# A two-layer encoder on one core: splitting the second output weights in the first attention, and multiplying part of the second output projection under the last head

## The chip, the cores and the metric

The kernel is one program on one core of a Trainium2 chip. The metric is device time in microseconds, from start to end of one execution; the median of three runs is 2327.5 us (2325.5 to 2328.0).

## The reference

One sequence of 1024 tokens with 1024 features passes two layers. Each layer is a token mixer and a SwiGLU feed-forward block, each followed by a residual and a layer norm. Layer 0 mixes with multi-head latent attention (8 heads), layer 1 with differential attention (8 heads, two softmax maps each). Both are masked by chunks of 64 tokens.

```
h = x
# layer 0
h = layernorm(ALPHA * h + mla_mixer(h) )          # ends with  o @ mla_w_o
h = layernorm(ALPHA * h + swiglu(h))
# layer 1
#   a = softmax(q0 k0) - lam * softmax(q1 k1);  o = a @ v, per head
#   o = rmsnorm(o, g_sub) * (1 - lambda_init)
h = layernorm(ALPHA * h + o @ diff_w_o)
h = layernorm(ALPHA * h + swiglu(h))
```

All is float32; the output must agree with a float32 computation.

## The kernel before

**Products.** Each float32 operand is split into an upper half `h`, its value rounded to float32r (a cast on ScalarE), and a lower half `l`, the rest (a subtraction on VectorE or GpSimd). A product is three float32r matmuls: `h*h`, `h*l`, `l*h`. `load_w` (L133 to L138) does this for weights: it loads 512 KB into a raw tile of the ring `wr` (two buffers), casts to `wh` and subtracts to `wl` (three buffers each). These rings serve all weights of the attentions.

**Order.** The program is written as a list of steps. A planner at compile time orders the instructions of every engine: it runs a model of the machine, and whenever an engine is free in it, the ready instruction that stands earliest in the program is placed next (some steps are raised in priority). On the chip each engine then takes its instructions in that fixed order; waits are by semaphore. Tiles come from pools of fixed buffers. A tile whose pool is full waits until an older tile's last reader is done.

**Attention.** `attention` runs over 64 steps, 8 heads by 8 blocks of 128 query tokens; the last head takes its blocks in the order 6, 7, 4, 5, 2, 3, 0, 1 (`LAST_ORDER`). At step b it issues `score` for step b + 2 (scores on TensorE, bias and row minimum on VectorE at L220, exponential on ScalarE at L223, scaling on GpSimd at L1024 or L1164, in layer 1 the combination of the two maps on VectorE at L1165), `turn` (transposes on TensorE at L149 and the split of their result at L244 and L245), every second step `mix` (probabilities times values, L256), and then whatever the table `fill` holds for that step. `fill` holds the projections of the next head, so that TensorE has work between the dependent steps of a block. The last head has no next head; its `fill` holds only the per-head norms (`norm_b`, `norm_b2`, L1189 to L1201). In layer 1 a head's normed output goes to DRAM (`o_dr`, L1204), except the last head's, which stays in the tile `bo`.

**Output projection.** `out_proj` loads and splits the eight heads' weights (6 in own tiles, 2 in the rings, for layer 1). Then, for each block of 128 tokens in `LAST_ORDER`, it fetches the block's head outputs from `o_dr` (`of`, L308), scales and splits them (L316, L317), loads the residual input (`z`, L320), multiplies two halves of 512 columns with 24 matmuls each (L144 to L146), adds them to `ALPHA * z` with row sums (L328), normalizes (`layer_norm`, L167 to L185), and transposes the block before for the feed-forward stage (`raw_x`). In layer 1 the split input `oh` and the pair `zy` (z and the normed y) are tiles of the ring `big`, which has five buffers of 1 MB. In the second attention these hold two query tiles, two key tiles and `bo`. As `out_proj` comes after `attention` in the program, the planner places its weight splits early, as soon as buffers are free, and its products when all seven stored heads of a block are in DRAM.

**After it** comes the feed-forward stage: gate and up products first (`gates`, which need the transposed first four blocks), with weights split in the rings.

Of the kernel before, what the change touches and what calls it, by code (L numbers as in the profile page):

```python
# [9 lines left out]
F32 = mybir.dt.float32  # L10
# [6 lines left out]
P = 128  # L17
# [25 lines left out]
def trunk(  # L43
# [82 lines left out]
    def small(name, n=1):  # L126
        return sp.tile([P, 2], F32, tag="small", name=name, bufs=22)[:, :n]

    def load_w(src, cols, name, hi=None, lo=None, eng=None, raw=None):

        if raw is None:
            raw = wp.tile([P, 1024], F32, tag="wr", bufs=2, name=f"r_{name}")
        nc.sync.dma_start(raw[:, :cols], src)  # L133
        if hi is None:
            hi = wp.tile([P, 1024], F32R, tag="wh", name=f"h_{name}")
            lo = wp.tile([P, 1024], F32R, tag="wl", name=f"l_{name}")
        A.copy(hi[:, :cols], raw[:, :cols])
        (eng or G).tensor_tensor(lo[:, :cols], raw[:, :cols], f32(hi[:, :cols]), ALU.subtract)  # L138
        return hi, lo
# [11 lines left out]
    def bcast_row(pool, src, n, name, tag):  # L151
        t = pool.tile([P, n], F32, tag=tag, name=name, bufs=1)
        nc.gpsimd.dma_start(t, src.partition_broadcast(P))
        return t
# [121 lines left out]
                fn()  # L276
        mix(blocks[-1][0], blocks[-1][1] // 2)

    def out_proj(side, w_o, o_dram, x_src, x_dst, lng, lnb, xo, layer, scale=None, last=None):


        with tc.tile_pool(name=f"op{layer}", bufs=2, side=side, reuse_waits="tile") as pool:
            g = bcast_row(pool, lng, D, f"mg{layer}", "g")
            b = bcast_row(pool, lnb, D, f"mb{layer}", "b")
            in_big, in_ring = ((0, 1, 2, 3, 7), (4, 5)) if layer == 0 else ((), (6, 7))
            wo = []
            for h in range(H):
                dst = ()
                if h in in_big:
                    t = big_tile(f"wo{layer}_{h}")  # L290
                    dst = (t[:, 0], t[:, 1])
                elif h not in in_ring:
                    t = pool.tile([P, 2, D], F32R, tag=f"wo{h}", name=f"wo{layer}_{h}", bufs=1)
                    dst = (t[:, 0], t[:, 1])
                wo.append(load_w(w_o[h], 1024, f"wo{layer}_{h}", *dst))

            def pair(name, dt, tag):
                if layer:
                    return big_tile(name, dt)
                return pool.tile([P, 2, D], dt, tag=tag, name=name)  # L300

            prev = None
            for tb in LAST_ORDER:
                nm = f"a{layer}_{tb}"
                of = pool.tile([P, H, P], F32, tag="of", name=f"of_{nm}", bufs=2)
                n = H if last is None else H - 1
                src = o_dram[tb // 2][:n, :, (tb % 2) * P:(tb % 2) * P + P]
                nc.sync.dma_start(of[:, :n], src.rearrange("h p q -> p h q"))  # L308
                ot = pair(f"oh_{nm}", F32R, "oh").rearrange("p a (h q) -> p a h q", h=H)
                oh, ol = ot[:, 0], ot[:, 1]  # L310
                if scale is None:
                    A.copy(oh, of)
                    V.tensor_tensor(ol, of, f32(oh), ALU.subtract)
                else:
                    for hs, o in ((slice(0, H - 1), of[:, :H - 1]), (H - 1, last(tb))):
                        A.activation(oh[:, hs], o, AF.Copy, scale=scale)  # L316
                        V.scalar_tensor_tensor(ol[:, hs], o, scale, f32(oh[:, hs]), ALU.mult, ALU.subtract)  # L317
                zy = pair(f"zy_{nm}", F32, "zy")
# [12 lines left out]
                if tb == LAST_ORDER[-1] and not layer:  # L331
                    y = big_tile(f"y_{nm}", F32)[:, 0]
                layer_norm(z, sums, junk, y, g, b, nm, x_dst[tb * P:(tb + 1) * P, :])
                if prev is not None:
                    raw_x(prev[1], xo, prev[0], f"a{layer}_{prev[0]}")
                prev = (tb, y)
        return lambda: raw_x(prev[1], xo, prev[0], f"a{layer}_{prev[0]}")

    def raw_x(y, xo, tb, name):

# [30 lines left out]
    def split(dst, src, eng):  # L371
        hi, lo = dst
        A.copy(hi, src)  # L373
        eng.tensor_tensor(lo, src, f32(hi), ALU.subtract)  # L374
# [436 lines left out]
        return new, rest, normed  # L811

    o_dr = [[dr.tile([H, P, 256], F32, name=f"o_dr{l}_{g}") for g in range(4)] for l in range(2)]
    xs_dr = [dr.tile([S, D], F32, name=f"xs_dr{l}") for l in range(3)]


# [120 lines left out]
    with ast as st:  # L937
# [64 lines left out]
        def k_nope(h, hf):  # L1002
# [9 lines left out]
            A.copy(kh[:, hs], m)  # L1012
            V.tensor_tensor(kl[:, hs], m, f32(kh[:, hs]), ALU.subtract)

        def score_a(h, i):
            hf, c = i // 4, slice((i % 4) * P, (i % 4) * P + P)
            (qh, ql), (kh, kl), qq = qn[h, hf], kn[h], qr[h, hf]
            l, r = softmax_block(
                lp,
                [(qh[:, c], kh), (qh[:, c], kl), (ql[:, c], kh), (qq[:, c], kr1), (qq[:, c], kr2)],  # L1020
                ba, i, MLA_SCALE, f"a{h}_{i}",
            )
            n = (i + 1) * P
            G.tensor_scalar(l[:, :n], l[:, :n], r, 1.0, ALU.mult, ALU.mult)  # L1024
            lt[h, i] = l
# [13 lines left out]
        def at(slot, fn, *args):  # L1039
            fill.setdefault(slot, []).append(lambda: fn(*args))  # L1040
# [21 lines left out]

    banks("ps2", PS_BUFS)
# [14 lines left out]
        return new_xT(pool, "f0")  # L1078

    xo, stacks = x_pools("m0", "right")  # L1080
    pending = out_proj("left", w_o_a, o_dr[0], x, xs_dr[0], ln_mix_g[0], ln_mix_b[0], xo, 0)
    xT, rest, normed = ffn("left", xo, stacks, pending, 0, xs_dr[0], xs_dr[1], ln_ffn_g[0], ln_ffn_b[0], next_x)


    banks("ps3", PS_BUFS_B)
    with ExitStack() as st:
# [104 lines left out]
        def norm_b2(h, g0=0, g1=4):  # L1191
            parts = []
            for i, (sq, o) in enumerate(sqs.pop((h, g0))):
                m = ps_s(f"ms{h}_{g0}_{i}")[:, :sq.shape[1]]
                T.matmul(m, ones, sq, start=True, stop=True)
                parts.append((sq, o, m))
            for r, _, m in parts:
                A.activation(r, m, AF.Ln, bias=eps_rms, scale=1.0)
            for r, o, _ in parts:
                A.activation(r, r, AF.Exp, scale=-0.5)  # L1200
                G.tensor_tensor(o, o, r, ALU.mult)  # L1201
            if h < H - 1:
                for g in range(g0, g1):
                    nc.sync.dma_start(o_dr[1][g][h], o_rows(h, g))  # L1204

# [39 lines left out]
        at(8 * H - 5, norm_b2, H - 1, 3, 4)  # L1245
        at(8 * H - 4, norm_b, H - 1, 2, 3)
        at(8 * H - 3, norm_b2, H - 1, 2, 3)
        attention(score_b, turn_b, mix_b, fill, 2, (0, 60))
        norm_b(H - 1, 0, 2)
        norm_b2(H - 1, 0, 2)  # L1250

    xst.close()
    xo, stacks = x_pools("m1", "left")
    pending = out_proj("right", w_o_b, o_dr[1], xs_dr[1], xs_dr[2], ln_mix_g[1], ln_mix_b[1], xo, 1, gs, last_rows)
# [91 lines left out]
```

## Time and profile before

| | us |
|---|---|
| median of three runs | 2327.5 (2325.52 to 2328.03) |
| profiled execution, its own time | 2323.21 |
| its span, first to last instruction | 2321.4 |
| TensorE busy | 2255.9 |
| VectorE, ScalarE, GpSimd busy | 1556.4, 1017.1, 891.7 |

The stages on the span's clock, from the timeline: first attention from about 100 to 365, first output projection and feed-forward to about 1105, second attention to 1587 (its last head from about 1525), second output projection to 1670, second feed-forward to the end. The granted clock of TensorE is 0.991 of full speed on average.

A row of a group reads: line, engine, operation, output from input, shapes and count, then durations. "[3.08 <-DVE mx_b L220]" behind a row means that the engine was idle for 3.08 us ahead of it, and what ended that. A row of waits reads: engine and tile that waited, what it waited for, then total us, count and longest. PE is TensorE, DVE VectorE, ACT ScalarE, POOL GpSimd, SP the queue that issues most transfers.

### The profile page before, as it was taken

Reading aid. Unit: us, or ns where it says so; the run is one execution under the profiler, and the core shown is the slowest. Engines: PE = TensorE matmul, PEld = TensorE weight load, DVE = VectorE, ACT = ScalarE, POOL = GpSimd, SP = SyncE. Lnnn points to the kernel's source line nnn. Section 1 sums busy time; section 2 is a strip of 40 time slices with the busy share of each in tenths; the row PEclk is TensorE's granted clock in tenths of the full one; section 3 lists DMA queues with packets and bytes.
Section 4 is the critical chain, followed back from the end, with each engine's and each line's share of the span. In section 5 each row is a group of like instructions: output and inputs, shape, how many; then the busy total and the mean of one; then the engine's idle time right before and its main releaser. Section 6 shows DMA issues by size and latency. Waiting matters only on the chain. (4 is left out here: it accounts for less than half of the span.)

```text
span 2321.4 us, 31073 instructions
## 1 busy us (share of the span) xinstructions
PE 2255.9 (97%) x11410; PEld 1922.3 (83%) x11410; DVE 1556.4 (67%) x2872; ACT 1017.1 (44%) x2089; POOL 891.7 (38%) x696
## 2 busy tenths in 40 slices
PE   7999999999999999999999999989999999999997
PEld 7899997888888887888888898867888888887886
DVE  4566765596666668767476666575596656658777
ACT  4355664352333324445365656564442333324353
POOL 3122342004444455555432424261014444436564
PEclk9999999999999999999999999989999999999999
DMA  5001124344313138454220212133334322337453
GB/s 201 9 28 37 40 71 169 104 164 145 136 68 136 69 118 321 183 185 154 91 55 19 69 37 69 37 110 129 134 138 149 105 99 106 109 131 301 148 198 124
DMA packets 100346, 272.56 MB, mean 117 GB/s; under 512 B 7504, under 2 KB 31184, under 8 KB 90464
## 3 DMA queue, kind: packets, MB, share of 16 engines
q1 hardware_dynamic: 95776, 260.14, 31.7%
q0 software_dynamic: 4416, 10.42, 1.7%
q8 instruction: 90, 1.47, 0.2%
q14 instruction: 64, 0.52, 0.1%
HBM read 197.13 MB, written 69.21 MB: 115 GB/s over the span
## 5 line engine op out<-in xcount | busy, mean ns | idle before, releaser
L373 ACT CAST op_g<-gr 128x512 fp32r<-128x512 f32 x240 | 147.5, 622 | 410.6 <-PE gb L418 229.7
L374 POOL TENSOR_TENSOR op_g<-gr,op_g 128x512 fp32r<-128x512 f32 x104 | 145.9, 1409 | 303.5 <-DVE tmp L509 153.5
L374 DVE TENSOR_TENSOR op_h<-rh,op_h 128x512 fp32r<-128x512 f32 x154 | 162.5, 1085 | 70.3 <-ACT op_h L373 70.3
L418 PE MATMUL ga<-xh_m,op_g 128*128 128x512 f32 x512 | 168.0, 389 | 0.0
L373 ACT CAST op_h<-rh 128x512 fp32r<-128x512 f32 x154 | 92.7, 619 | 145.5 <-DMA rh<-h_dr 38.2
L686 PE MATMUL dw<-op_w_t,op_h 128*128 128x512 f32 x660 | 151.3, 390 | 0.0
L686 PEld LDWEIGHTS dw<-op_w_t,op_h 128*128 128x128 f32 x660 | 123.6, 188 | 25.8 <-DVE op_h L374 0.3
L374 POOL TENSOR_TENSOR op_w_t<-tt,op_w_t 128x512 fp32r<-128x512 f32 x66 | 99.3, 1508 | 79.3 <-ACT op_w_t L373 79.3
L223 ACT ACTIVATE l_b<-l_b,mx_b 128x256 f32<-128x256 f32 (+7 forms) x128 | 99.5, 777 | 69.0 <-DVE mx_b L220 66.9
L686 PE MATMUL dx<-op_w_b,op_h 128*128 128x512 f32 x528 | 122.4, 391 | 6.1 <-ACT op_w_b L373 3.9
L686 PEld LDWEIGHTS dx<-op_w_b,op_h 128*128 128x128 f32 x528 | 98.4, 188 | 29.8 <-ACT op_w_b L373 4.7
L1164 POOL TENSOR_SCALAR l_b<-l_b,r_b,cst 128x128 f32<-128x128 f32 (+3 forms) x64 | 53.0, 827 | 178.5 <-DVE r_b L225 169.7
L418 PE MATMUL gb<-t4h_f,op_g 128*128 128x512 f32 x352 | 115.9, 390 | 3.4 <-DVE tmp L501 3.4
L418 PE MATMUL gc<-b22h_f,op_g 128*128 128x512 f32 x352 | 115.6, 389 | 1.3 <-ACT op_g L373 1.3
L374 DVE TENSOR_TENSOR op_g<-gr,op_g 128x512 fp32r<-128x512 f32 x136 | 109.6, 807 | 9.4 <-ACT op_g L373 9.0
L418 PE MATMUL gc<-t1h_f,op_g 128*128 128x512 f32 x352 | 115.5, 389 | 0.0
L418 PE MATMUL gb<-t3h_f,op_g 128*128 128x512 f32 x352 | 115.2, 389 | 0.0
L418 PE MATMUL gb<-t2h_f,op_g 128*128 128x512 f32 x352 | 114.8, 389 | 0.0
L418 PEld LDWEIGHTS ga<-xh_m,op_g 128*128 128x128 f32 x512 | 96.1, 188 | 19.9
L374 POOL TENSOR_TENSOR op_g<-s,op_g 128x512 fp32r<-128x512 f32 x40 | 55.6, 1391 | 142.9 <-ACT op_g L373 142.9
L144 PE MATMUL bp<-xT_f,h_wb 128*128 128x512 f32 x256 | 102.8, 402 | 0.0
L146 PE MATMUL bp<-xT_f,l_wb 128*128 128x512 f32 x256 | 101.6, 397 | 0.0
(350 smaller groups left out, 6833.8 us busy)
## 6 DMA issues: line engine op xcount, KB each, us to landing
gr<-in_w_gu SPq DMA_DIRECT2D x44, 1024.0 KB, 6.7
rh<-h_dr SPq DMA_DIRECT2D x28, 1024.0 KB, 5.1
h_dr<-sh SPq DMA_DIRECT2D x22, 1024.0 KB, 4.9
h_dr<-hp SPq DMA_DIRECT2D x22, 768.0 KB, 4.1
tt<-in_w_dn SPq DMA_DIRECT2D x22, 512.0 KB, 8.2
rh<-h_dr SPq DMA_DIRECT2D x14, 768.0 KB, 4.5
z<-xs_dr SPq DMA_DIRECT2D x16, 512.0 KB, 10.6
rw_b<-in_w_dn SPq DMA_DIRECT2D x8, 1024.0 KB, 8.9
```

What stands on the lines that cost most here:

```text
L144: T.matmul(ps_out, lh, rh, start=(i == 0), stop=False)
L146: T.matmul(ps_out, ll, rh, start=False, stop=(i == n - 1))
L223: A.activation(l[:, :n], l[:, :n], AF.Exp, bias=mx, scale=-1.0, accum_out=sm)
L373: A.copy(hi, src)
L374: eng.tensor_tensor(lo, src, f32(hi), ALU.subtract)
L418: T.matmul(o, w[:, a, kc], x[b][:, k, :], start=(first and k == 0 and (a, b) == (0, 0)), stop=(k == 3 and a == 1), skip_group_check=True,)
L686: T.matmul(o, h[:, a, c], w[:, b_], start=(first and (a, b_) == (0, 0)), stop=(last and a == 1), skip_group_check=True,)
L1164: G.tensor_scalar(l1[:, :n], l1[:, :n], r1, nlam, ALU.mult, ALU.mult)
```

## The change

1. **Weights of the second output projection.** `split_wo(h)` is put into the first attention's `fill`, one per head (steps 5, 13, ... 53, and 44 for the last): it loads and splits one head's weights through the same rings, and writes both halves to DRAM (`wo_dr`, 1 MB a head). Later they are loaded as finished operands, by GpSimd's queue.
2. **`out_proj`** serves layer 0 alone. For layer 1 there is a class `OutProj`. It is opened at step 54 of the second attention, when the projections are done and the transposed input is released: it issues eight heads' operand loads and fetches the first block's six heads.
3. **Early products.** For the first two blocks (6 and 7) the products of heads 0 to 5 are put into the last head's `fill`: `early` for block 6 at steps 56, 57 and 58 (two heads each), for block 7 at steps 60 and 61 (three heads each). Their sums are added to `ALPHA * z` at once; heads 6 and 7 follow in `late`, at step 63 for block 6, which adds them with the row sums.
4. **Heads 6 and 7 stay on the core** in `bo` (before, head 7 alone), so `o_dr` has six heads.
5. **Buffers.** For the first two blocks the split inputs lie in the weight rings (block 6) and an own tile (block 7), and z in the `wr` ring, where y overwrites it. For the other six blocks `oh` and `zy` are tiles of `big`, as before. The norm's scale and shift, before two tiles of `out_proj`'s pool, are one tile of `big` (`gb1`).

The core of the diff (the cuts in `out_proj` for layer 1's options are left out):

```diff
+    class OutProj:
+        HEADS = H - 2
+        def __init__(self, side, w_dr, o_dram, o_here, x_src, x_dst, scale):
...
+            self.of(LAST_ORDER[0])
+            for h in range(H):
+                if h < self.HEADS:
+                    t = self.pool.tile([P, 2, D], F32R, tag=f"wo{h}", name=f"wo1_{h}", bufs=1)
+                    nc.gpsimd.dma_start(t, w_dr[h])
...
+                else:
+                    t = [wp.tile([P, D], F32R, tag=f"w{p}", name=f"w{p}o1_{h}") for p in "hl"]
+                    for p in range(2):
+                        nc.gpsimd.dma_start(t[p], w_dr[h][:, p])
...
+        def of(self, tb):
+            nm, n = f"a1_{tb}", self.HEADS
+            of = self.pool.tile([P, n, P], F32, tag="of", name=f"of_{nm}")
...
+            nc.sync.dma_start(of, src.rearrange("h p q -> p h q"))
+            first = tb in LAST_ORDER[:2]
+            if tb == LAST_ORDER[0]:
+                hl = [wp.tile([P, D], F32R, tag=f"w{p}", name=f"o{p}_{nm}") for p in "hl"]
+            elif first:
+                t = self.pool.tile([P, 2, D], F32R, tag="oh", name=f"oh_{nm}", bufs=1)
...
+            else:
+                t = big_tile(f"oh_{nm}")
...
+            self.split(tb, slice(0, n), of)
+            if first:
+                z = wp.tile([P, D], F32, tag="wr", name=f"z_{nm}", bufs=2)
+                self.z[tb] = (z, z)
+            else:
+                zy = big_tile(f"zy_{nm}", F32)
...
+            nc.sync.dma_start(self.z[tb][0], self.x_src[tb * P:(tb + 1) * P, :])
...
+        def early(self, tb, heads):
+            for nh in range(2):
+                self.product(tb, nh, heads, heads[-1] == self.HEADS - 1)
+            if heads[-1] == self.HEADS - 1:
+                for nh in range(2):
+                    self.added(tb, nh, ALPHA, False)
+                    del self.m[tb, nh]
+
+        def late(self, tb):
+            self.split(tb, slice(self.HEADS, H), self.o_here(tb))
+            first = tb in LAST_ORDER[:2]
+            for nh in range(2):
+                self.product(tb, nh, range(self.HEADS if first else 0, H), True)
+                self.added(tb, nh, 1.0 if first else ALPHA, True)
+
+        def rest(self, lng, lnb, xo):
+            gb = big_tile("gb1", F32)
+            for i, src in enumerate((lng, lnb)):
+                nc.gpsimd.dma_start(gb[:, i], src.partition_broadcast(P))
+            prev = None
+            for tb in LAST_ORDER:
+                if tb not in LAST_ORDER[:2]:
+                    self.of(tb)
+                if tb != LAST_ORDER[0]:
+                    self.late(tb)
+                z, y = self.z[tb]
+                layer_norm(z, self.sums[tb], [self.m[tb, nh] for nh in range(2)], y, gb[:, 0], gb[:, 1],
+                           f"a1_{tb}", self.x_dst[tb * P:(tb + 1) * P, :])
+                if prev is not None:
+                    raw_x(self.z[prev][1], xo, prev, f"a1_{prev}")
+                prev = tb
...
+        def split_wo(h):
+            for p, t in enumerate(load_w(w_o_b[h], 1024, f"pwo{h}")):
+                nc.sync.dma_start(wo_dr[h][:, p], f32(t))
...
+            at(b + 5, split_wo, h - 1)
+        at(8 * H - 20, split_wo, H - 1)
...
-            return ob[:, (H - 1) % 2, tb * P:(tb + 1) * P]
+            return ob[:, :, tb * P:(tb + 1) * P]
...
-            if h < H - 1:
+            if h < H - 2:
...
+        b = 8 * (H - 1) - 2
+        at(b, begin_out)
+        for slot, what, args in (
+            (2, "early", (first, (0, 1))), (3, "early", (first, (2, 3))), (4, "early", (first, (4, 5))),
+            (4, "of", (second,)), (6, "early", (second, (0, 1, 2))), (7, "early", (second, (3, 4, 5))),
+            (9, "late", (first,)),
+        ):
+            at(b + slot, lambda what, *a: getattr(proj[0], what)(*a), what, *args)
```

More of the change, by code (lines that the diff above doesn't have):

```diff
@@ L277, in attention, with out_proj @@
         mix(blocks[-1][0], blocks[-1][1] // 2)
[L279 to L285, printed above, removed]
+    def out_proj(side, w_o, o_dram, x_src, x_dst, lng, lnb, xo):
+        with tc.tile_pool(name="op0", bufs=2, side=side, reuse_waits="tile") as pool:
+            g = bcast_row(pool, lng, D, "mg0", "g")
+            b = bcast_row(pool, lnb, D, "mb0", "b")
             wo = []
@@ L288, in out_proj @@
                 dst = ()
-                if h in in_big:
-                    t = big_tile(f"wo{layer}_{h}")
+                if h in (0, 1, 2, 3, 7):
+                    t = big_tile(f"wo0_{h}")
                     dst = (t[:, 0], t[:, 1])
-                elif h not in in_ring:
-                    t = pool.tile([P, 2, D], F32R, tag=f"wo{h}", name=f"wo{layer}_{h}", bufs=1)
+                elif h == 6:
+                    t = pool.tile([P, 2, D], F32R, tag=f"wo{h}", name=f"wo0_{h}", bufs=1)
                     dst = (t[:, 0], t[:, 1])
[L295 to L300, printed above, removed]
+                wo.append(load_w(w_o[h], 1024, f"wo0_{h}", *dst))
             prev = None
             for tb in LAST_ORDER:
-                nm = f"a{layer}_{tb}"
+                nm = f"a0_{tb}"
                 of = pool.tile([P, H, P], F32, tag="of", name=f"of_{nm}", bufs=2)
[L306 to L309, printed above, removed]
+                src = o_dram[tb // 2][:, :, (tb % 2) * P:(tb % 2) * P + P]
+                nc.sync.dma_start(of, src.rearrange("h p q -> p h q"))
+                ot = pool.tile([P, 2, D], F32R, tag="oh", name=f"oh_{nm}").rearrange("p a (h q) -> p a h q", h=H)
                 oh, ol = ot[:, 0], ot[:, 1]
[L311 to L318, printed above, removed]
+                A.copy(oh, of)
+                V.tensor_tensor(ol, of, f32(oh), ALU.subtract)
+                zy = pool.tile([P, 2, D], F32, tag="zy", name=f"zy_{nm}")
                 z, y = zy[:, 0], zy[:, 1]
@@ L330, in out_proj @@
                     )
-                if tb == LAST_ORDER[-1] and not layer:
+                if tb == LAST_ORDER[-1]:
                     y = big_tile(f"y_{nm}", F32)[:, 0]
@@ L813, in trunk @@
     o_dr = [[dr.tile([H, P, 256], F32, name=f"o_dr{l}_{g}") for g in range(4)] for l in range(2)]
+    wo_dr = [dr.tile([P, 2, D], F32, name=f"wo_dr{h}") for h in range(H)]
     xs_dr = [dr.tile([S, D], F32, name=f"xs_dr{l}") for l in range(3)]
@@ L1080, in trunk @@
     xo, stacks = x_pools("m0", "right")
-    pending = out_proj("left", w_o_a, o_dr[0], x, xs_dr[0], ln_mix_g[0], ln_mix_b[0], xo, 0)
+    pending = out_proj("left", w_o_a, o_dr[0], x, xs_dr[0], ln_mix_g[0], ln_mix_b[0], xo)
     xT, rest, normed = ffn("left", xo, stacks, pending, 0, xs_dr[0], xs_dr[1], ln_ffn_g[0], ln_ffn_b[0], next_x)
@@ L1247, in trunk, with begin_out @@
         at(8 * H - 3, norm_b2, H - 1, 2, 3)
+        first, second = LAST_ORDER[:2]
+        proj = []
+        def begin_out():
+            xst.close()
+            proj.append(OutProj("right", wo_dr, o_dr[1], last_rows, xs_dr[1], xs_dr[2], gs))
+        b = 8 * (H - 1) - 2
[6 more added lines that the diff above has]
+            at(b + slot, lambda what, *a: getattr(proj[0], what)(*a), what, *args)
         attention(score_b, turn_b, mix_b, fill, 2, (0, 60))
@@ L1250, in trunk @@
         norm_b2(H - 1, 0, 2)
-    xst.close()
     xo, stacks = x_pools("m1", "left")
-    pending = out_proj("right", w_o_b, o_dr[1], xs_dr[1], xs_dr[2], ln_mix_g[1], ln_mix_b[1], xo, 1, gs, last_rows)
+    pending = proj[0].rest(ln_mix_g[1], ln_mix_b[1], xo)
     banks("ps4", PS_BUFS)
```

41 lines of the change are left out of this document (39 added, 2 removed).

## The prediction

> **What bounds the kernel now.** I read the page's first table, then a table by stage, then in the stage that the change touches what TensorE waited for, and last the timeline of each engine there.
>
> ```profile
> PE 2255.9 (97%) x11410; PEld 1922.3 (83%) x11410; DVE 1556.4 (67%) x2872; ACT 1017.1 (44%) x2089; POOL 891.7 (38%) x696
> ```
>
> TensorE is busy for 2255.9 of 2321.4 us, so 65.5 us of idle time are all that better filling could win, plus what a lowered clock costs. The table by stage shows the columns busy time and count of PE, weight loads, DVE, ACT and POOL, then the granted clock, the DMA share and GB/s:
>
> ```profile
> core 0: us, PE busy (x) PEld busy (x) DVE busy (x) ACT busy (x) POOL busy (x), PEclk, DMA share, GB/s
> 150.00:350.00 200.00, 200.00 (x1310) 183.39 (x1309) 140.25 (x402) 122.99 (x310) 68.36 (x64) 1.00 0.14 45
> 1525.00:1575.00 50.00, 37.34 (x176) 29.31 (x176) 40.26 (x107) 36.46 (x84) 33.38 (x22) 0.83 0.52 166
> 1530.00:1535.00 5.00, 4.92 (x22) 3.33 (x20) 3.92 (x11) 4.42 (x9) 4.24 (x3) 0.70 0.26 91
> 1540.00:1545.00 5.00, 4.32 (x25) 4.06 (x23) 2.69 (x12) 3.34 (x8) 2.60 (x3) 0.68 0.40 119
> 1545.00:1550.00 5.00, 2.56 (x11) 2.28 (x12) 4.54 (x8) 2.20 (x4) 4.90 (x2) 0.66 0.33 105
> 1550.00:1555.00 5.00, 5.00 (x28) 5.00 (x28) 4.19 (x9) 4.58 (x10) 3.23 (x3) 0.66 0.32 105
> 1570.00:1575.00 5.00, 4.49 (x13) 3.63 (x14) 4.37 (x12) 4.67 (x13) 1.19 (x2) 0.66 0.88 312
> 1575.00:1670.00 95.00, 95.00 (x457) 79.24 (x456) 48.70 (x99) 32.15 (x70) 7.88 (x11) 1.00 0.28 97
> ```
>
> The first attention (150 to 350) and the second output projection (1575 to 1670) have no idle TensorE at all. The last head of the second attention (1525 to 1575), which has no projections left to mix in, has 50 - 37.34 = 12.7 us idle. In the five slices with a low clock the busy time is also stretched: 4.92 x 0.30 + 4.32 x 0.32 + (2.56 + 5.00 + 4.49) x 0.34 = 7.0 us. So 19.7 us are lost in this stage. What TensorE waited for there:
>
> ```profile
> PE s_b L217 <- DVE mx_b L220: 4.0, 3, 3.1
> PE pt_b L149 <- DVE l_b L1165: 3.6, 2, 2.4
> PE s_b L217 <- DVE bk L1150: 2.0, 1, 2.0
> ```
>
> All three end on VectorE, which is busy 40 of 50 us. Two of its operations explain most of it. The combination of the two softmax maps on L1165 is one instruction per block; of the three between 1530 and 1546 (min/median/max ns):
>
> ```profile
> L1165 DVE SCALAR_TENSOR_TENSOR l_b<-l_b,r_b,l_b x3: 1279/3040/3223, 1530.2 to 1544.9; 128x1024 f32<-128x1024 f32 x2, 128x896 f32<-128x896 f32 x1
> ```
> ```profile
> 1534.86 3.22 DVE L1165 SCALAR_TENSOR_TENSOR l_b<-l_b,r_b,l_b 128x896 f32<-128x896 f32 x1 [0.45 <-POOL l_b L1164]
> ```
> ```profile
> 1538.80 0.42 PE L217 MATMUL s_b<-bk,bq 128*128 128x320 f32 x1 [3.08 <-DVE mx_b L220]
> ```
>
> One took 1.28 us for 1024 columns, the others 3.04 and 3.22 (for fewer columns); the 3.1 us wait is a score that needs the bank's maximum queued behind the 3.22. Beside them GpSimd forms the lower halves of the output weights:
>
> ```profile
> L138 POOL TENSOR_TENSOR wo<-r_wo,wo x6: 2331/2366/2982, 1523.6 to 1544.5; 128x1024 fp32r<-128x1024 f32 x6
> L138 POOL TENSOR_TENSOR l_wo<-r_wo,h_wo x2: 2404/2808/3213, 1546.9 to 1552.8; 128x1024 fp32r<-128x1024 f32 x2
> ```
> ```profile
> L137 ACT CAST wo<-r_wo x6: 1044/1046/1050, 1522.4 to 1543.3; 128x1024 fp32r<-128x1024 f32 x6
> L137 ACT CAST h_wo<-r_wo x2: 1029/1046/1063, 1545.8 to 1551.6; 128x1024 fp32r<-128x1024 f32 x2
> ```
>
> The first product of the output projection comes only near the end, since its input needs head 6 back from DRAM:
>
> ```profile
> 1570.51 0.80 PE L144 MATMUL zp_a<-wo,oh_a 128*128 128x512 f32 x1 [0.86 <-ACT oh_a L316]
> ```
>
> **The change part by part.** (a) The eight weight splits leave the last head. That takes 8 x 1.05 = 8.4 us from ScalarE and 6 x 2.4 + 2 x 2.8 = 20 us from GpSimd. On TensorE's path I count the excess of the two long operations, 3.22 + 3.04 - 2 x 1.28 = 3.7 us, and half of the 2.0 us wait for bk, whose cast stands behind weight casts on ScalarE: 4.7 us. With those gaps goes the low clock behind them, 40 to 45, 45 to 50 and 50 to 55: 4.32 x 0.32 + 7.56 x 0.34 = 4.0 us. I take 8 of these 8.7; at worst nothing, if the next wait in line is as late.
>
> The Trainium skill (SBUF — State Buffer, Who interferes with whom) says that a VectorE instruction with two SBUF inputs and a GpSimd instruction that reads SBUF exclude each other for a whole instruction. The 3.22 beside 1.28 us agrees.
>
> (b) Two blocks x two halves x six heads x three = 72 matmuls move under the last head. Their pitch, from two successive block boundaries (eight transposes, then 48 matmuls):
>
> ```profile
> 1609.60 1.03 PE L149 MATMUL xTp_a<-ident,zy_a 128*128 128x128 f32 x8
> ...
> 1621.37 1.03 PE L149 MATMUL xTp_a<-ident,zy_a 128*128 128x128 f32 x8
> ```
>
> (11.77 - 1.03) / 48 = 0.224 us, so 72 cost 16.1 us. They win only where they stand in idle time. After (a), 19.7 - 8.7 = 11 us of loss are left. Some of it lies before 1532, where no weights are in yet (below), and the order is fixed ahead, so not every gap gets its product. Bounds 0 and 11; I take 5. The splits and sums that come with them (four more additions into z on VectorE) lie on VectorE in place of the 3.7 us that it no longer stalls.
>
> (c) The big ring has five buffers. During the second projection one holds the last heads' outputs, and now one the norm's scale and shift (before, these had their own tiles). Three instead of four are left for each block's split input and its z/y pair. Before, a block's input was split one block ahead; with three, it must wait until the block before is multiplied. TensorE then has only the eight transposes to do. The old trace has one such case, at the first change of blocks:
>
> ```profile
> 1590.08 1.05 ACT L316 ACTIVATE oh_a<-of_a,cst 128x896 fp32r<-128x896 f32 x1 [1.67 <-PE zp_a L146]
> ```
> ```profile
> 1591.16 1.15 DVE L317 SCALAR_TENSOR_TENSOR oh_a<-of_a,cst,oh_a 128x896 fp32r<-128x896 f32 x1
> ...
> 1613.25 1.14 DVE L317 SCALAR_TENSOR_TENSOR oh_a<-of_a,cst,oh_a 128x896 fp32r<-128x896 f32 x1
> ```
>
> There the lower half was done at 1592.31, 2.2 us after the release. Less 1.0 us of transposes and two matmuls that need only the upper half (0.4), 0.8 us stay open. At the later boundary (1609.60) VectorE took it up behind the norm and the transposes' copies and ended at 1614.39, 4.8 us behind, which would leave 3.4 us. There are four such boundaries (before the third to sixth of the remaining six blocks). I take 1 us each, near the first row since the wait is of its kind: 4 us, with bounds of 3 and 14 before any loss of clock.
>
> By the rows a gap of 2.4 us is followed by a clock of 0.66 in two slices (45 to 55), while 1575 to 1670 keeps 1.00. The Trainium skill (TensorE: Matmul & The Clock Gate, Part 1) has the clock fall only after an idle window of about 3.4 us; by that the gaps of (c) would lose no clock, and the sum would stay as it is. The rows differ: gaps of 2.0 to 3.1 us did it here.
>
> (d) In the first attention eight splits and eight 1 MB stores are added. TensorE is full there, so only a late operand can hurt:
>
> ```profile
>   PE pt_a L149: 0.3, 1
> ```
> ```profile
> ACT h_wa L137 <- PE kn L145: 5.0, 4, 2.5
> ```
>
> The first row (who waited for the first attention's probabilities) shows 0.3 us of TensorE waiting on GpSimd's scaling in the whole stage: a split of 2.4 us ahead of it on the queue is mostly covered by scores that run two blocks ahead. The second row shows that casts of the next head's weights already wait for a free buffer of the three-deep ring, which the new splits now share; head weights come later, into a margin of several blocks. On SyncE a store waits for GpSimd, and the head's output store and the next weight load queue behind it; outputs have two buffers. Bounds 0 and 8 x 2.4 = 19 us (nothing covered); I take 3. Below nothing is excluded, as nothing there leaves.
>
> (e) The weights' loads are on GpSimd's queue and wait, as the old scale's load did, for the last projection:
>
> ```profile
> 1522.21 0.59 POOL L153 DMA_DIRECT2D mg<-in_ln_mix_g  x1 [3.77 <-PE bp L146]
> ```
> ```profile
> q0 software_dynamic: 4416, 10.42, 1.7%
> ```
>
> Ten issues of 0.59 us are 6 us in front of the softmax scaling, less than the splits they replace. That row gives packets, MB and the share of 16 engines: 10.42 MB in 0.017 x 16 x 2321 = 631 us of engine time, 264 GB/s over 16 engines: 4.0 us for a head's 1.05 MB. Heads 0 and 1 land near 1531, 2 and 3 near 1539, 4 and 5 near 1547, each about a block ahead of the point where the program places their products. No cost.
>
> The sum: -8 - 5 + 4 + 3 = -6 us. The profiled execution took 2323.2 us (span 2321.4 and 1.8 around it), 4.3 below the median of the runs shown; so 2317.2 in a profile like it and 2321.5 as a median. A measurement of this kernel can tell about 0.2%, 4.7 us, from no change.
>
> **The rivals.** *Slower: the ring of three.* If each of the four boundaries costs the later row's 3.4 us plus, at two of them, 2 us of clock, (c) is 18 instead of 4: +8, 2335.5. It decides once a boundary costs more than (13 - 3) / 4 = 2.5 us. For it: three tiles cannot hold two blocks' inputs and z pairs, and VectorE prefers the older norm work. Against: the row at 1591. The next stage's gate products could fill the last boundaries, but need all of the first four blocks transposed.
>
> *Weights late.* If the fixed order puts the first early products into the first gap (about 1526), they wait for weights until 1531, and scores and transposes wait behind them, as TensorE takes its queue in order. The 5 us of (b) go and 4 are added: +3, 2330.5. For it: ScalarE waited for weight loads already. Against: the program has these products two blocks later. The Trainium skill (SBUF — State Buffer, the "DVE blocks DMA" trap) says that loads issued from GpSimd can starve while VectorE runs in a two-port mode; no run here shows it yet.
>
> *Early products that are not early.* If they end up behind the attention's own work, (b) is 0: -1, 2326.5.
>
> **How the numbers follow.** Forecast 0.50, ring of three 0.22, weights late 0.18, not early 0.10. Within the forecast, (b) from 2 to 9 and (d) from 0 to 6 give -12 to 0: 0.39 faster, 0.11 within 0.2%. The ring gives 0.20 slower, 0.02 same. Late weights: 0.02 faster, 0.08 same, 0.08 slower. Not early: 0.04 same, and 0.06 slower where (d) is above its middle. Together 0.41 faster, 0.25 same, 0.34 slower. The range goes from 2311, where (a) and (b) win 16 and (c) and (d) cost 5, to the ring's 2336. The forecast's own range is 2315 to 2327.
>
> **What would show it.** Right: L1165 at most 1.3 us throughout the last head; zp products from about 1532 on; that stage under 8 us of loss; gaps of about 1 us at four boundaries of the projection, clock 1.00. Wrong: TensorE waiting on a weight load under the last head; gaps of 3 us and a clock near 0.66 between 1590 and 1660; idle TensorE or a longer span in the first attention.

## The result, and the profile after

The change made the kernel slower by 0.3%: 2332.1 us (2331.1 to 2337.6), beside 2326.0 us for the kernel before, ratio 1.003 with a 95% interval of 1.0021 to 1.004. The forecast was 2321.5 us. The profiled execution has a span of 2331.5 us (before 2321.4), with TensorE as busy as it was:

```profile
PE 2254.7 (97%) x11410; PEld 1918.7 (82%) x11410; DVE 1556.9 (67%) x2876; ACT 1017.4 (44%) x2089; POOL 894.8 (38%) x706
```

So the 10 us are idle time of TensorE (2331.5 - 2254.7 = 76.8 us instead of 65.5). The table by stage, with the columns of the prediction's table, over 50 us of the last head (1527 to 1577), two slices of it, and the second output projection (1589 to 1677):

```profile
core 0: us, PE busy (x) PEld busy (x) DVE busy (x) ACT busy (x) POOL busy (x), PEclk, DMA share, GB/s
1527.00:1577.00 50.00, 34.59 (x189) 29.43 (x188) 29.70 (x82) 20.31 (x46) 11.84 (x17) 0.83 0.61 221
1537.00:1542.00 5.00, 0.00 (x0) 0.00 (x0) 0.00 (x0) 0.00 (x0) 2.32 (x3) 0.67 1.05 398
1542.00:1547.00 5.00, 0.00 (x0) 0.00 (x0) 0.00 (x0) 0.00 (x0) 0.54 (x1) 0.50 1.08 409
1589.00:1677.00 88.00, 84.80 (x389) 67.92 (x389) 49.83 (x107) 34.45 (x78) 9.66 (x13) 0.98 0.33 114
```

For ten microseconds three engines do nothing at all, while the transfer engines are full (share 1.05 to 1.08, about 400 GB/s). Of the waits between 1518 and 1600 these name the chain:

```profile
ACT oh_a L378 <- DMA of_a<-o_dr: 15.0, 1, 15.0
PE s_b L217 <- DVE mx_b L220: 14.4, 1, 14.4
DVE oh_a L379 <- ACT oh_a L378: 13.8, 1, 13.8
PE zp_a L390 <- DMA wo<-wo_dr: 0.6, 1, 0.6
```

Read from the end: a score on TensorE waits for a row minimum on VectorE; VectorE stands at the lower half of a split, which waits for its upper half on ScalarE; ScalarE waits for the load `of_a` of a token block's head outputs. The weights, which the prediction watched, cost 0.6 us. ScalarE's timeline shows which block it is:

```profile
1531.25 0.94 ACT L378 ACTIVATE oh_a<-of_a,cst 128x768 fp32r<-128x768 f32 x1
1547.17 0.93 ACT L378 ACTIVATE oh_a<-of_a,cst 128x768 fp32r<-128x768 f32 x1 [14.98 <-DMA of_a<-o_dr]
```

These are the splits of block 6 and block 7, one directly behind the other in ScalarE's fixed order. In the program block 7's fetch stands four steps after block 6's; the planner moved it up. The two loads were issued on SP 0.5 us apart, and landed after 3.6 and 19.1 us:

```profile
L355 SPq DMA_DIRECT2D of_a<-o_dr x2: 371/454/538, 1527.6 to 1528.1; - x2
DMA to landing us min/median/max: 3.6/11.3/19.1
```

Between the two, at 1527.9, GpSimd began to issue the weights. The queues from 1528 to 1552 (packets, MB, share of 16 engines; q0 is GpSimd's, q1 SP's):

```profile
q0 software_dynamic: 1339, 8.04, 83.5%
q1 hardware_dynamic: 2077, 1.05, 18.3%
```

A weight packet took 0.835 x 16 x 24 / 1339 = 0.24 us, a packet of SP's queue (505 B on average, nearly all of them `of_a`'s 512 B) 0.034 us. Block 7's load is 128 x 6 such pieces, 48 for each of 16 engines if they are shared out evenly.

The other loss is in the first attention. The first product of the first output projection starts at 373.6 instead of 364.9.

### The profile page after: what moved, and what is told of

It is laid out like the page before. It is cut to its first block, busy times and chain, and to the rows that moved or that the text cites. A ratio compares the mean times of both kernels' runs of the same rounds, so it can differ in the third digit from the quotient of the medians.

```text
span 2331.5 us, 31115 instructions
## 1 busy us (share of the span) xinstructions
PE 2254.7 (97%) x11410; PEld 1918.7 (82%) x11410; DVE 1556.9 (67%) x2876; ACT 1017.4 (44%) x2089; POOL 894.8 (38%) x706
## 5 line engine op out<-in xcount | busy, mean ns | idle before, releaser
L471 POOL TENSOR_TENSOR op_w_t<-tt,op_w_t 128x512 fp32r<-128x512 f32 x66 | 98.7, 1499 | 78.7 <-ACT op_w_t L470 76.8
```

## The experiments

Each ran in five rounds beside the kernel before. "End of A" is the start of the first product of the first output projection; "last stage" runs from the start of the last `bp` matmul (before the last head) to that of the last `zp` matmul of the second projection. Both come from one profile of each kernel; stages that an edit doesn't touch differ between these profiles too (see below).

| kernel | median, us | ratio to before (95%) | end of A | last stage |
|---|---|---|---|---|
| before | 2325.2 to 2326.9 | 1 | 364.9 | 146.7 |
| changed | 2332.1 | 1.0030 (1.0021 to 1.0040) | 373.6 | 149.7 |
| e1_of_first | 2323.4 | 0.9987 (0.9976 to 0.9998) | 374.1 | 138.8 |
| e5_layout | 2319.0 | 0.9972 (0.9963 to 0.9981) | 371.8 | 135.4 |
| e11_half | 2324.7 | 1.0005 (0.9995 to 1.0015) | 370.4 | 142.1 |
| e13_pin7 | 2318.9 | 0.9963 (0.9950 to 0.9977) | 372.1 | 133.5 |
| e2_split_only | 2329.6 | 1.0013 (1.0004 to 1.0023) | 372.6 | 146.3 |
| e8_no_store | 2329.3 | 1.0018 (1.0010 to 1.0027) | 369.9 | 146.8 |
| e3_ffn_split | 2329.4 | 1.0009 (1.0000 to 1.0018) | 365.1 | 149.6 |
| e7_gp_store | 2318.8 | 0.9970 (0.9958 to 0.9982) | 366.0 | 139.1 |
| e9_pin | 2315.5 | 0.9954 (0.9942 to 0.9966) | 367.5 | 135.4 |
| e10_layout_gp | 2319.1 | 0.9974 (0.9965 to 0.9983) | 366.6 | 135.1 |
| e12_layout_ffn | 2314.9 | 0.9961 (0.9949 to 0.9973) | 366.3 | 134.9 |
| e4_both | 2318.9 | 0.9962 (0.9948 to 0.9976) | 366.1 | 138.9 |
| e6_no_early | 2323.0 | 0.9994 (0.9985 to 1.0003) | 363.7 | 140.3 |
| e14_two_pins | 2313.0 | 0.9941 (0.9928 to 0.9953) | 368.8 | 133.6 |

**The gap under the last head.** First the load was put ahead of the weights.

```diff
-            nc.sync.dma_start(of, src.rearrange("h p q -> p h q"))
+            (nc.gpsimd if tb == LAST_ORDER[0] else nc.sync).dma_start(of, src.rearrange("h p q -> p h q"))
```

> One load, the first token block's attention outputs of_a, is issued on GpSimd's queue ahead of the weights instead of on SP's beside them. Theory (the last head's 14.4 us gap is that load starved by the weight loads: it took 15 to 17 us in the changed kernel, 6 us where nothing competes): it lands within about 7 us of its issue near 1528, the gap at the scores and the slow clock at 1540 to 1555 go, and the time falls by 14 to 18 us, to 2314 to 2318. Rival (the transfer engines are full until the weights are in, or ScalarE waits for something else): the gap moves or stays, 2328 to 2333. The first attention is untouched in both: last score there still near 359.6 against 353.8 before.

Measured: 8.7 us less than the changed kernel, the gap gone. The expectation had the wrong block: block 6's load was never slow. Moving it left SP's queue free for block 7's, issued at 1529.7, before the first weight (1530.9); the two landed in 4.3 and 3.3 us. The gain fell short of 14. The profile shows that the weights came later, that one early product waited for them, and that the clock fell behind it. The first row is from TensorE's timeline, the others from the table by stage:

```profile
1538.09 2.05 PE L390 MATMUL zp_a<-wo,oh_a 128*128 128x512 f32 x4 [2.52 <-DMA wo<-wo_dr]
```
```profile
1537.00:1542.00 5.00, 3.91 (x9) 3.14 (x10) 3.79 (x12) 2.52 (x5) 1.11 (x2) 0.50 1.06 406
1542.00:1547.00 5.00, 5.00 (x22) 4.02 (x21) 3.45 (x9) 1.26 (x3) 1.27 (x3) 0.84 1.08 408
```

The wait and the busy time that the clock stretched come to 2.5 + 3.91 x 0.50 + 5.00 x 0.16 = 5.3 us.

Next, the load stayed beside the weights and its piece size changed, by another layout of `o_dr[1]`: for each group, `[2, P, H, P]` (3 KB a partition) or `[2, H // 2, P, 2, P]` (1 KB), instead of `[H, P, 256]`. The later blocks' loads change with it, and the stores of the heads' outputs, before 1 KB a partition, become pieces of 512 B in both.

```diff
-            nc.sync.dma_start(of, src.rearrange("h p q -> p h q"))
+            nc.sync.dma_start(of, self.o_dram[tb // 2][tb % 2][:, :n])
```

> The changed kernel with only the layout of the second attention's outputs in DRAM altered, so that a block's of_a load reads one run of 3 KB for each partition instead of six of 512 B; it stays on SP's queue beside the weights, and the splits stay in the first attention. Theory (the transfer engines take a packet from each queue in turn, so a load of 48 short packets an engine waits behind 48 weight packets of about 0.3 us): with 8 packets an engine it lands about 8 x (0.3 + 0.1) + 2 = 5 to 7 us after its issue, the 14.4 us gap goes, and the time is that of the kernel with of_a on GpSimd's queue, 2321 to 2326. Rival (the engines work off the weights before they come to it, whatever its packets are): it still takes 15 us or more, 2330 to 2334.

> The changed kernel with of_a in runs of 1 KB (two heads together) instead of 512 B or 3 KB, all else as it was. Theory (one packet from each queue in turn): 24 packets an engine beside weight packets of 0.3 us each give 24 x 0.36 + 2 = 9 to 11 us from issue to landing, between the 17 us of 512 B and the 4.4 us of 3 KB; the gap at the scores is then 4 to 8 us and the time 2323 to 2328. Rival (512-B runs alone are slow, and anything longer is fast): 4 to 6 us, 2319.

Measured, the two loads of each kernel (3 KB, then 1 KB); the larger figure is block 7's:

```profile
L354 SPq DMA_DIRECT2D of_a<-o_dr x2: 332/378/425, 1526.7 to 1527.1; - x2
DMA to landing us min/median/max: 3.0/4.2/5.3
```
```profile
L355 SPq DMA_DIRECT2D of_a<-o_dr x2: 359/420/482, 1523.5 to 1524.0; - x2
DMA to landing us min/median/max: 3.0/7.2/11.4
```

8, 24 and 48 pieces an engine landed in 5.3, 11.4 and 19.1 us: 0.38 and 0.32 us more for each further piece, somewhat over one weight packet and one own packet, 0.24 + 0.03. The bytes are the same in all three. So here the load did not wait for all weights ahead of it, and not its size but its count of pieces set its time. The gap followed. With 3 KB no wait of TensorE over 1.6 us is left there; with 1 KB its timeline has

```profile
1538.84 0.79 PE L217 MATMUL s_b<-bk,bq 128*128 128x512 f32 x1 [6.97 <-DVE mx_b L220]
```

Both theories held and the rivals (full queue; only 512 B slow) fell; two sizes lay just outside, the landing with 1 KB (11.4 us, expected 9 to 11) and the time with 3 KB (2319.0, expected 2321 to 2326). The Trainium skill (DMA: Bandwidth & Descriptors, Queues, rings and completion order) says that an engine takes its queues in turn, a packet at a time, and gives a packet as some 9 to 17 descriptors. The taking in turn agrees; the runs come near one weight piece for each of the load's own, and cannot show how many go together.

Last, the slow load was kept and the split moved: on ScalarE and VectorE block 7's split was held behind the last `pth` copy and `ptl` subtraction of block 4, as the program has it.

```diff
-            A.activation(oh, o, AF.Copy, scale=self.scale)
-            V.scalar_tensor_tensor(ol, o, self.scale, f32(oh), ALU.mult, ALU.subtract)
+            c = A.activation(oh, o, AF.Copy, scale=self.scale)
+            d = V.scalar_tensor_tensor(ol, o, self.scale, f32(oh), ALU.mult, ALU.subtract)
+            if tb == LAST_ORDER[1] and hs.start == 0:
+                _, hc, lc = turned[-1]
+                behind(c.ins, hc)
+                behind(d.ins, lc)
```

> The changed kernel, its loads and layout untouched, with one thing held: the split of block 7's of_a on ScalarE and VectorE comes behind the last copy and subtraction of block 4's transposes, where the program has it, instead of directly behind block 6's split. Theory (the slow load costs only because a split that waits for it stands in ScalarE's fixed order ahead of the attention's work): block 7's load still takes 15 to 20 us, but lands before its split's turn; no gap over 3 us in the last head, 2332 - 13 = 2319, 2317 to 2322. Rival (the load's lateness is what counts: the gap only moves, to block 7's early products or to the next blocks' loads behind it on the queue): 2326 to 2332.

Measured: 2318.9 us. The load is as slow as before, the split comes at 1560.7, and the stage keeps its clock:

```profile
L357 SPq DMA_DIRECT2D of_a<-o_dr x2: 370/454/538, 1527.7 to 1528.2; - x2
DMA to landing us min/median/max: 3.5/11.9/20.2
```
```profile
1560.70 0.94 ACT L380 ACTIVATE oh_a<-of_a,cst 128x768 fp32r<-128x768 f32 x1
```
```profile
1525.00:1575.00 50.00, 45.78 (x262) 38.04 (x262) 37.53 (x110) 30.46 (x72) 16.57 (x22) 1.00 0.61 221
```

So the loss needs both: a load that 48 turns beside the weights make slow, and a split that waits for it ahead of the attention's work in an engine's fixed order. Either alone cost next to nothing: in e5 the split stood as early, and waited 1.1 us.

**The first attention.** `e2_split_only` is the kernel before with `split_wo` and its stores, `e8_no_store` the same without the stores, `e3_ffn_split` the changed kernel with the splits moved.

```diff
-            at(b + 5, split_wo, h - 1)
...
+            if layer == 0 and i >= 40 and (i - 40) % 12 == 0 and (i - 40) // 12 < H:
+                j = (i - 40) // 12
+                for p, t in enumerate(load_w(w_o_b[j], 1024, f"pwo{j}")):
+                    nc.sync.dma_start(wo_dr[j][:, p], f32(t))
```

> The kernel before, with only the first attention's part added: each head's second output weights are loaded, split and stored to DRAM there (nobody reads them). Theory (the first attention is where the other 8.7 us went): last score there near 359 instead of 353.8, first product of the first output projection near 373 instead of 365, and the whole 5 to 9 us longer, 2331 to 2335. Rival (the prediction's term of +3, and the rest from elsewhere): 2328 to 2330.

> The kernel before with the splits in the first attention, but without the 16 stores: load, split, and nothing more. Theory (the stores on SP's queue are what costs): the first product of the first output projection near 366 to 367 instead of 372.6, the whole as the kernel before, 2325 to 2327. Rival (the splits themselves cost, by ring and engines): near 372, 2329 to 2330.

> The changed kernel, with the splitting of the second output weights moved out of the first attention into the first feed-forward layer's stream of weight tiles (one head's after every 12th tile). Theory (the splits cost because they crowd the first attention and the run-up to the first output projection): last score of the first attention back near 353.8, the whole 8 us shorter than the changed kernel, near 2324, the 14.4 us gap in the last head still there. Rival (the splits' cost goes with the work wherever it is put: each is 1.1 us of VectorE and 1.1 us of ScalarE time and 2 MB of transfers): no shorter than 2330.

Measured: `e2_split_only` is 3.7 us longer than the kernel before by the medians, as the rival (the prediction's +3) said, although its first attention ends 7.7 us later. In its profile some 3 us come back in the second attention, which the edit doesn't touch: from the first `bv` to the last `bp` matmul it takes 417.7 us there and in the changed kernel, 420.8 in the profile of before (and 420.7 in that of `e8_no_store`). The clock of 1100 to 1150 differs, before, then changed:

```profile
1100.00:1150.00 50.00, 46.00 (x295) 42.53 (x293) 26.07 (x45) 19.97 (x42) 20.85 (x17) 0.93 0.27 90
```
```profile
1100.00:1150.00 50.00, 46.08 (x317) 42.28 (x316) 30.17 (x55) 22.57 (x49) 19.83 (x16) 1.00 0.26 83
```

In all sixteen profiles this stage goes with that clock: 417.7 to 417.8 us where it is 1.00, 418.9 to 419.3 at 0.97, 420.7 and 420.8 at 0.93. In the last feed-forward layer, which the edit doesn't touch either, the profile of `e2_split_only` loses 3.8 us again (645.1 against 641.3 us from the last `zp` to the last `dw` matmul). So stages of single profiles can't be added up to a difference of medians.

Without the stores nothing was won in the median, against the theory. Moved into the feed-forward layer the splits leave the first attention at its old length (365.1), but lengthen that layer by 3.1 us; 2.8 us less in all where 8 were expected.

The profiles show where a part of it lies. From the last score of the first attention (of `kn` and `qh`; the last of all starts 0.3 to 0.4 us later) to the first product of the projection it is 11.1 us in before, e3, e4 and e7, and 13.7 to 14.5 in the changed kernel, e1, e2, e5, e8, e11 and e13, with and without stores. ScalarE's timeline there, before and changed (rows of L1034 and L1137 left out), then VectorE's in the changed kernel:

```profile
358.43 0.69 ACT L244 CAST pth_a<-pt_a 128x256 fp32r<-128x256 f32 x2
359.02 1.05 ACT L312 CAST oh_a<-of_a 128x1024 fp32r<-128x1024 f32 x1
...
360.53 0.37 ACT L244 CAST pth_a<-pt_a 128x256 fp32r<-128x256 f32 x1
```
```profile
364.54 1.04 ACT L303 CAST oh_a<-of_a 128x1024 fp32r<-128x1024 f32 x1 [0.65 <-DMA of_a<-o_dr]
365.49 0.36 ACT L244 CAST pth_a<-pt_a 128x256 fp32r<-128x256 f32 x1
...
366.02 0.28 ACT L244 CAST pth_a<-pt_a 128x128 fp32r<-128x128 f32 x1
366.55 0.37 ACT L244 CAST pth_a<-pt_a 128x256 fp32r<-128x256 f32 x1 [0.26 <-PE pt_a L149]
369.19 0.38 ACT L244 CAST pth_a<-pt_a 128x256 fp32r<-128x256 f32 x1 [2.27 <-DVE ptl_a L245]
```
```profile
365.62 3.21 DVE L304 TENSOR_TENSOR oh_a<-of_a,oh_a 128x1024 fp32r<-128x1024 f32 x1 [1.41 <-ACT oh_a L303]
368.75 1.28 DVE L245 TENSOR_TENSOR ptl_a<-pt_a,pth_a 128x256 fp32r<-128x256 f32 x4
```

It is an engine's order again: with the splits added the planner put a split that waits for a load ahead of four of the attention's copies, where it stood ahead of one, and its lower half on VectorE likewise. Here the load itself cost only 0.65 us; the attention's subtractions stood mostly behind the lower half, 3.21 us long. `e9_pin` is `e5_layout` with that split held behind them.

```diff
+                if tb == LAST_ORDER[0]:
+                    for i, hc, lc in turned[-8:]:
+                        if i in (0, 2, 3):
+                            behind(c.ins, hc)
+                            behind(d.ins, lc)
```

> The kernel with 3-KB runs for of_a and the splits in the first attention, stores on SP, with one thing more: the first output projection's first split (oh_a of block 6, which waits for a load) is held behind the first attention's last copies and subtractions of pth and ptl on ScalarE and VectorE, where the kernel before has it; in the changed kernel the planner put it three copies ahead of them. Theory (14.0 us from the last score to the first product of the first output projection in the kernels with that order, 11.1 us in those with the old one, whatever the splits do): 11.1 us in that stretch and about 3 us less in all, 2316 against 2319. Rival (the stretch is long because the weights' splits come late there): 14 us still, 2319.

Measured: the stretch is 10.2 us, the time 2315.5, 3.5 less than `e5_layout`. So of the splits' cost about 3 us are that order in this pair; between the profiles of `e13_pin7` and `e14_two_pins` below, which differ in it alone, the end of A comes 3.3 us earlier, and the median is 5.9 us shorter. The stores were also put on GpSimd's queue (`nc.gpsimd.dma_start(wo_dr[h][:, p], f32(t))` in `split_wo`), in `e7_gp_store` (over `e1_of_first`) and `e10_layout_gp` (over `e5_layout`), and the splits into the feed-forward layer over `e5_layout`.

> The kernel with of_a ahead of the weights and the splits in the first attention, with the 16 stores of the halves issued on GpSimd's queue instead of SP's. Theory (the splits cost because the stores wait on SP's queue and the attention's own weight loads and output stores wait behind them): the first attention is back near its old length, the first product of the first output projection near 366 to 368, and the time 2316 to 2319 against 2323.4. Rival (the splits cost by their work on ScalarE and GpSimd and by the ring of weight tiles): 2321 to 2326.

> 3-KB runs for of_a, and the 16 stores of the halves on GpSimd's queue (the order at the end of the first attention is then the old one without being held). If the gains add up: 2319.0 - 4.6 = 2314.4, 2311 to 2317. If the stores' gain is only the order's 3 us: 2316.

> 3-KB runs for of_a, and the splits in the first feed-forward layer instead of the first attention. If the gains add up: 2319.0 - 4.5 = 2314.5, 2311 to 2317; if the splits cost the same there: 2319.

Measured: `e7_gp_store` is 4.6 us under `e1_of_first`; it has the old order, so its theory of the queue is not shown by it. `e10_layout_gp` is no faster than `e5_layout`, though its profile has the short stretch and an end of A 5.2 us earlier; what took that back is open. `e12_layout_ffn` came out as the sum had it.

**The early products**, and the combinations. `e4_both` has the edits of e1 and e3. `e6_no_early` is `e4_both` without the calls of `early`, and with all heads in `late`:

```diff
-                self.product(tb, nh, range(self.HEADS if first else 0, H), True)
-                self.added(tb, nh, 1.0 if first else ALPHA, True)
+                self.product(tb, nh, range(H), True)
+                self.added(tb, nh, ALPHA, True)
```

> Both edits at once: the first of_a load ahead of the weights on GpSimd's queue, and the splits in the first feed-forward layer. If both causes hold and add up: 2332 - 15 - 8 = about 2308, 2304 to 2312, faster than both kernels. If the gap is filled by another wait, 2316 to 2324; if the splits cost as much in the feed-forward layer, 2314 to 2318.

> The kernel with both edits (of_a ahead of the weights, splits in the feed-forward layer) without the early products: the first two token blocks multiply all eight heads after the attention, as the others do. Theory (the prediction's terms: the 72 early products fill idle time worth 5 us): about 5 us longer than with them, 2324, bounds 0 to 11. Rival (the last head is bound by the softmax chain so that the products come into time that is otherwise lost entirely: 72 x 0.23 = 16 us): 2335. Rival on the other side (they delay scores as much as they fill): 2317 to 2320.

> The changed kernel with both orders held: block 7's split in the last head, and the first output projection's first split at the end of the first attention. If each does alone what it did elsewhere: 2332 - 13 - 3.5 = 2315.5, 2313 to 2319, faster than both kernels with no transfer changed.

Measured: `e4_both` 2318.9, faster than both kernels, but 13.3 us under the changed one where 23 were expected: the two edits alone had brought 8.7 and 2.8. `e6_no_early` doesn't test what its expectation says: the planner moved block 6's products up into the last head all the same. The matmuls into `zp_a`, in `e4_both`, then in `e6_no_early` (columns PE, weight loads, DVE and ACT), and those of block 6's lower half `ol_a` in `e6_no_early`:

```profile
1525.00:1570.00 45.00, 20.49 (x72) 14.43 (x72) 2.06 (x3) 0.00 (x0) 0.92 0.67 246
```
```profile
1525.00:1550.00 25.00, 11.70 (x36) 7.87 (x36) 0.00 (x0) 0.00 (x0) 0.86 1.07 397
1525.00:1570.00 45.00, 14.63 (x48) 10.04 (x48) 0.00 (x0) 0.00 (x0) 0.92 0.66 242
```
```profile
L390 PE MATMUL zp_a<-wo,ol_a x12: 387/395/628, 1532.4 to 1549.3; 128*128 128x512 f32 x12
```

One product in three is of `ol_a`, so all 36 of block 6 were done by 1550, and only block 7's 36 came later. It is 4.1 us longer by medians, 0.32% (7 us) by ratios. Only 1.4 of that lie in the last stage; from the last `zp` to the last `dw` matmul its profile has 650.9 us against 642.0, which the edit doesn't touch. So block 7's early products are worth something between 1 and 7 us, and what block 6's are worth no run shows. `e14_two_pins`, the change with two orders held and no transfer altered, has the lowest median: 2313.0 us, 0.6% under the kernel before and 19 us under the change as it was made; its interval overlaps with those of `e9_pin` and `e12_layout_ffn`.

## Why the prediction was wrong

**(e), "No cost", is the step that failed.** It asked when the weights land and not what they do to other transfers. They came faster than its estimate (379 GB/s from 1528 to 1552, all queues together, against 264), and TensorE waited for them 0.6 us; but they made block 7's load slow (19.1 us), which none of the terms costed, and the prediction placed the early products by the program without asking where the planner could move the split ahead of them. That split stopped TensorE for 14.4 us. Without the wait (`e13_pin7`, `e5_layout`) the kernel measures 2318.9 and 2319.0, some 13 us less than the change as it was made. Beside 2326.9 and 2325.2 that is 8.0 and 6.2 us faster, where the sum said 6. That they come so near is in part luck: by their profiles the end of the first attention is 7.2 and 6.9 us later, not 3, and the last feed-forward layer, which no term counts, 6.7 and 2.9 us longer than before.

**(a) to (c)**, together -9: -13.2 and -11.3 in the last stage (133.5 and 135.4 against 146.7), of one profile each. The long combinations went, as forecast:

```profile
L1270 DVE SCALAR_TENSOR_TENSOR l_b<-l_b,r_b,l_b x10: 342/1084/1284, 1524.2 to 1596.4; 128x896 f32<-128x896 f32 x2, 128x1024 f32<-128x1024 f32 x2, 128x640 f32<-128x640 f32 x1, 128x768 f32<-128x768 f32 x1
```

(b): the first early product came at 1534.1, where "about 1532" was said; its 5 us were tested only for block 7. (c), sized 4, was about 1.3: the idle time in the four slices of the changed kernel that hold it, with the clock at 1.00:

```profile
1620.00:1630.00 10.00, 9.85 (x48) 7.83 (x47) 4.28 (x10) 3.12 (x7) 0.00 (x0) 1.00 0.37 140
1640.00:1650.00 10.00, 9.80 (x43) 7.85 (x43) 6.15 (x11) 4.15 (x10) 0.55 (x1) 1.00 0.42 144
1650.00:1660.00 10.00, 9.51 (x45) 7.41 (x44) 5.50 (x11) 3.23 (x7) 0.55 (x1) 1.00 0.29 104
1660.00:1670.00 10.00, 9.51 (x45) 7.45 (x44) 5.50 (x12) 3.23 (x7) 0.55 (x1) 1.00 0.15 55
```

So the ring of three, with +8 the rival nearest to the measured +6, did not happen.

**(d)**, +3, was 3.7 by the medians of `e2_split_only`. The size was right and the reasons were not the main thing: some 3 us of it are the changed order at the stage's end, which the prediction didn't foresee. How the rest divides between splits and stores isn't settled.

**The rival of late weights** came nearest in kind, an engine stopped by a wait in its fixed order, but it had TensorE waiting for the weights. The Trainium skill (SBUF — State Buffer, the "DVE blocks DMA" trap) lets loads issued from GpSimd starve while VectorE runs a two-port operation. The runs show nothing of it: GpSimd's loads had 83.5% of the engines' time and starved another load.

**The range** had a slip: 16 us won and 5 paid are 11 from 2327.5, which is 2316.5 and not 2311.

## What to carry to other kernels

When a change adds a large transfer, list the small loads that run beside it, count their pieces per transfer engine, and look what stands behind their first consumer on its engine. Long runs or a place ahead on the queue mend the load; holding the consumer back in the order mends the wait, and here that altered no transfer and was as good as the long runs. Where a planner orders the engines, any added work can move a waiting or a long instruction somewhere else, so compare the orders of both kernels around each load before a loss is put down to the added work.

## What the runs showed of the hardware that was not expected

A load of 384 KB took 19.1, 11.4 or 5.3 us beside weight packets of 6 KB on average (8.04 MB in 1339), as it was cut into 48, 24 or 8 pieces an engine; issued ahead of the first weight, loads of 48 pieces took 3.3 to 4.3 us (changed kernel and e1).

TensorE's clock: waits of 2.5 us (e1) and 2.8 us (e4) were each followed by a granted clock of 0.50 over five microseconds, while in e5 waits of 1.2, 1.5 and 1.5 us left it at 1.00 from 1520 to 1600. The length of one wait doesn't decide it alone: behind a wait of 1.5 us the changed kernel has 0.68 (1597 to 1602), where e5 keeps 1.00 behind one just as long (1582 to 1592). The Trainium skill (TensorE: Matmul & The Clock Gate, Part 1) has the clock fall after some 3.4 us of idleness; here waits of 1.5 to 2.8 us were enough.
